# Fewer attention steps beside the input projection's last block, and the second feed-forward product's sums in the first product's tiles

## The chip, the cores and the metric

The kernel runs on one core of a Trainium2 chip. The metric is the device time of one execution in microseconds (us). An execution has five engines that run their own instruction streams in order: TensorE (PE, with its weight loads as PEld), VectorE (DVE), ScalarE (ACT), GpSimd (POOL) and SyncE (SP). Here SP issues the transfers between HBM and the on-chip memory.

## What is computed

One layer of a hybrid decoder on 2048 tokens of width 1024, in float32:

```
h = rms_norm(x, mix_norm_g);  P = h @ w_in
A = sliding_window_attention(...)   # 6 heads, window 128, blocks of 128 queries
B = rwkv7_mixer(...)                # a recurrence over the sequence
M = memory_attention(...)           # 4 heads against 256 memory tokens
x = x + concat(A, B, M) @ w_out
u = rms_norm(x, ffn_norm_g) @ w_up               # 1024 -> 2 * 2816
uc = conv_b + sum(conv_w[i] * shifted(u, i))     # causal, width 3
gate, val = split(uc)
x = x + (silu(gate) * val) @ w_down              # 2816 -> 1024
```

## The kernel before

Every float32 product is made of three matmuls of split operands: high part by high part, high by low, low by high. ACT makes the high part by a cast (`whi<-wraw`, `h2h<-tr`), DVE the low part by a subtraction (`wlo<-wraw,whi`, `h2l<-tr,h2h`). The tokens are worked on transposed, in blocks of 512 columns.

**Order of the work.** The program isn't issued as it is written. `Recorder` (line 132) records every operation; `slots` (line 212) lets a tile that takes a ring's place wait for the users of the tile that it replaces; `order` (line 239) gives every operation a level, the length of the longest path from it to the end by a table of costs, and `run` (line 269) then lists the operations of each engine, the highest level first among those that are ready. So the order in which steps are recorded acts through the rings of tiles (above all the PSUM ring `ip` of two places, which attention shares with the projection's statistics and transposes), and through the opening and closing of pools.

**First half of the kernel.** `ip` (line 677) is the input projection: four blocks of 512 tokens, 17 projections each, every one 24 matmuls `mm<-hh,...` of 512 columns, so 68 projections, counted by g. After each one `side(g)` (line 1546) advances two generators. `rw` is RWKV: 4 steps for each of 16 tiles of 128 tokens, at the projections that `starts` names, with a chain of 31 small DVE steps in each tile (`xtmp`, `xinv`). `atn` is attention (line 904): six steps for each of 16 tiles, 96 in all. Its matmuls write `pl`, `tpa` and `po` (window), `plm`, `tpm` and `pm` (memory). It may start once `x_done` has run, behind the last projection of the third block; from g = 52 on, the formula with 72 advances it by 72 steps over the last block's 16 projections, 12 tiles. What is left of it is recorded behind the projection, one step of `atn` and one of `rw` in turn (`run`, line 1485). `outproj` (line 1266) is recorded last: four blocks of eight projections (`mm<-ch,...`), each block from the attention and RWKV results of four tiles, with `ch` and `cl` in one place each.

**Second half.** `feed_forward` (line 1435) splits the tokens into two halves of 1024 columns. A product of a pair of weight rows is made by `seven` (line 1379): seven block products (sums in PSUM `uf`, `uip`, `uch`) in place of eight, with operands prepared by `operands` (line 1345) and seven slots of activations, `h2h` and `h2l`. `ffn_up` (line 1393) makes 22 such products for each half; DVE adds their sums into `ub`, then ACT and DVE make the convolution in `uc`, and DVE the gated product and its combinations in `uc` and `tt`, which SP writes to HBM (`dg`). All of these lie in the pool `fu`: three places `ub` of 1026 columns, five `uc` of 1024. `ffn_down` (line 1426) makes the second product: SP reads `dg` back (`tr<-dg`) into the slots, three stages of four calls for each half, and DVE adds each sum into `acc`, which is first loaded from `dx2`, the layer's sum so far, and written to `out` at the end of a half. `acc` is one tile of 8 x 1024 columns in a pool of its own, opened after `fu` is closed.

Of the kernel before, what the change touches and what calls it, by code (L numbers as in the profile page):

```python
# [10 lines left out]
F32 = mybir.dt.float32  # L11
# [7 lines left out]
P = 128  # L19
SEQ = 2048  # L20
D = 1024
KC = D // P
# [7 lines left out]
HALF = 2 * BLK  # L30
# [99 lines left out]
class Recorder:  # L130
# [15 lines left out]
    def pool(self, name, bufs, space=None, side=None):  # L146
        p = Pool_(name, bufs, space, side)
        self.pools.append(p)
        p.op = self.barrier[space] = self._mark("open", p, [self.barrier[space]] if space in self.barrier else [])
        self.stacks.setdefault((space, side), []).append(p)  # L150
        return p
# [72 lines left out]
    def margin(self, d, o):  # L224

        return 0 if d.eng == o.eng or None in (d.eng, o.eng) else MARGIN

# [33 lines left out]
    def run(self):  # L261
# [35 lines left out]
        while True:  # L297
# [17 lines left out]
            if soon[e] and o.dur > 150:  # L315
                c = min((c for c in soon[e] if c[0] < t + min(WAIT, o.dur) and c[2].level > o.level), default=None)
                if c:
# [41 lines left out]


WAIT = 100
MARGIN = 300
SLACK = 1500
WR = 4
# [4 lines left out]
UB = 3  # L369
# [44 lines left out]
class K:  # L414
# [1011 lines left out]
    def ffn_down(self, i, k0, nk, slots, w1, w2, ps, acc):  # L1426

        lo, hi = slice(0, BLK), slice(BLK, HALF)
        m1, m2 = acc[:, i], acc[:, i + 4]
        to = [(m1[:, lo],), (m1[:, lo],), (m1[:, hi],), (m2[:, hi],), (m2[:, hi],), (m1[:, hi],), (m2[:, lo],)]  # L1430

        def use(s, o):
            for c in to[s]:
                self.nc.vector.tensor_tensor(out=c, in0=o, in1=c, op=ALU.add)
        self.seven(ps, self.operands(w1, w2, lambda c, q: self.a["w_down"][i + 4 * c][:, (k0 + nk * q) * P:(k0 + nk * (q + 1)) * P]),
                   slots, nk, use)

    def feed_forward(self, ps):
        rec, pool, nc = self.rec, self.rec.pool, self.nc
        up = pool("fu", 1, side="right")  # L1440
        self.ucar = up.tile([P, 2 * NFC, 2], F32, name="ucar")
        nc.vector.memset(self.ucar, 0.0)
        w1, w2, tr = pool("fw1", 3), pool("fw2", 3), pool("fr", 3)
        slots = self.slots
        short = lambda: up.tile([P, BLK], F32, name="tt", bufs=4)
        wide = lambda name: up.tile([P, HALF], F32, name="uc", bufs=5)
        back = lambda: tr.tile([P, BLK], F32, name="tr")
        order = [k0 + q * nk + k for k0, nk in STAGES for k in range(nk) for q in range(2)]
        for half in range(2):
            if half:  # L1450
                self.from_dram(slots, 4, lambda k: self.dh[k], back)
            for n, j in enumerate(order):
                u = self.ffn_up(j, slots, w1, w2, up, ps)
                if n % 2:
                    self.to_dram(self.dg[half][n // 2], first, u, short)
                first = u
                if half == 0 and n == 7:
                    for k, r in self.normalised(1, wide):
                        self.to_dram(self.dh[k], *r, short)
        rec.close(up)  # L1460
        ap = pool("acc", 1, side="right")
        acc = ap.tile([P, KC, HALF], F32, name="acc")
        for half in range(2):
            col = slice(half * HALF, (half + 1) * HALF)
            for kc in range(KC):
                nc.sync.dma_start(out=acc[:, kc], in_=self.dx2[kc, :, col])
            pair = 0
            for k0, nk in STAGES:
                self.from_dram(slots, nk, lambda k: self.dg[half][pair + k], back)
                pair += nk  # L1470
                for i in range(4):
                    self.ffn_down(i, k0, nk, slots, w1, w2, ps, acc)
            for kc in range(KC):
                nc.sync.dma_start(out=self.out[kc * P:(kc + 1) * P, col], in_=acc[:, kc])
        for q in (ap, tr, w2, w1):
            rec.close(q)


    def run(self):
        tc, rec = self.tc, self.rec  # L1480
# [18 lines left out]
        pool = rec.pool  # L1499
# [44 lines left out]
        atn = []  # L1544

        def side(g):
            for _ in range(starts.get(g, 0)):
                next(rw, None)
            if atn and (g - 52) * 72 // 16 >= 0:
                for _ in range((g - 51) * 72 // 16 - (g - 52) * 72 // 16):  # L1550
                    next(atn[0], None)
        for n, b in (("t", 2), ("w", 4), ("h", 1), ("x", 4)):
            p[n] = pool(n, b, side="right")
# [2 lines left out]
        def x_done():  # L1556
# [3 lines left out]
            p["a"] = pool("a", 2)  # L1560
            atn.append(self.attention(p, ps))
        self.ip(p, ps, side, x_done)
        for n in ("h", "w", "t"):
            rec.close(p[n])
# [12 lines left out]
        wide = lambda name: rp.tile([P, HALF], F32, name=name, bufs=1 if name == "bc" else 2)  # L1577
# [117 lines left out]
```

## Time and profile before

| | |
|---|---|
| time, median of 3 runs | 2493.63 us (2492.27 to 2495.86) |
| the profiled execution | 2499.48 us |
| its span, first to last instruction | 2497.6 us |
| PE busy | 2372.4 us (95%) |
| PEld busy | 1886.0 us (76%) |
| DVE busy | 2015.2 us (81%) |
| ACT busy | 1219.6 us (49%) |
| POOL busy | 190.2 us (8%) |

Busy shares are of the span. A matmul's busy time holds its pipeline's latency, so matmuls that follow each other closely overlap in it. The "granted clock" is the share of TensorE's full clock in a stretch. A row's last part in brackets says how long the engine was idle before it and what ended that. All operations are recorded on one line (L349), so rows are told apart by their tiles.

### The profile page before, as it was taken

What the parts mean: (1) busy time and instruction counts of PE and PEld (TensorE: products, weight loads), DVE (VectorE), ACT (ScalarE), POOL (GpSimd) and SP (SyncE); (2) the same over time, 40 slices, a digit from 0 to 9 for tenths busy, and PEclk for the clock granted to TensorE, in tenths of its full rate; (3) what the DMA queues carried; (4) which work ended last, traced back from release to release, by engine and by line L of the source; (5) the groups of instructions that cost most, each with busy time, mean ns of one, the idle gap of its engine ahead of it and who ended that gap; (6) DMA issues with size and microseconds to landing.
All of it is one profiled execution on the core that took longest, in us unless ns stands there. A gap on an engine that the chain in (4) does not pass through costs nothing.

```text
span 2497.6 us, 36689 instructions
## 1 busy us (share of the span) xinstructions
PE 2372.4 (95%) x12268; PEld 1886.0 (76%) x12268; DVE 2015.2 (81%) x4614; ACT 1219.6 (49%) x2413; POOL 190.2 (8%) x292
## 2 busy tenths in 40 slices
PE   8899989899899979999899999999999998999999
PEld 6677777676666757777788888888888876888887
DVE  7579677878878777759588998899888887888876
ACT  6354544555445544555355455565555463444442
POOL 1112212211111121100000000000000000000000
PEclk9999999899989989999999999999999998999999
DMA  7586746744434465557233733354323246558443
GB/s 226 176 246 179 214 127 176 190 131 137 138 106 132 118 192 157 168 162 238 81 117 110 261 119 117 115 179 137 106 93 113 100 150 214 162 155 275 148 141 129
DMA packets 292933, 389.30 MB, mean 156 GB/s; under 512 B 49911, under 2 KB 155392, under 8 KB 292744
## 3 DMA queue, kind: packets, MB, share of 16 engines
q1 hardware_dynamic: 292744, 386.96, 49.8%
q8 instruction: 97, 1.59, 0.3%
q14 instruction: 92, 0.75, 0.1%
HBM read 274.89 MB, written 111.97 MB: 155 GB/s over the span
## 4 chain that ended last, share of the span: by engine, by line
PE 80%; DVE 8%; DMA 7%; issue 3%; ACT 1%; SPq 0%; POOL 0%; POOLq 0%; DVEq 0%; ACTq 0%
PE uf L349 28%; PE mm L349 16%; PE uch L349 14%; PE uip L349 7%; PE pq L349 4%; PE po L349 2%; PE pg L349 1%; DMA nb<-nbd 1%; PE tpa L349 1%; DVE xtmp L349 1%; DVE wlo L349 1%; PE pl L349 1%; PE st L349 1%; DVE xinv L349 1%; DMA wraw<-w_down_in 1%
## 5 line engine op out<-in xcount | busy, mean ns | idle before, releaser
L349 ACT CAST whi<-wraw 128x512 fp32r<-128x512 f32 (+1 forms) x410 | 250.2, 613 | 423.7 <-PE uf L349 148.9
L349 PE MATMUL uf<-h2h,wlo 128*128 128x512 f32 x1056 | 412.2, 392 | 15.3 <-DVE wlo L349 15.3
L349 PE MATMUL uf<-h2h,whi 128*128 128x512 f32 x1056 | 412.7, 392 | 4.7 <-ACT whi L349 4.6
L349 PE MATMUL uf<-h2l,whi 128*128 128x512 f32 x1056 | 412.6, 391 | 0.0
L349 DVE TENSOR_TENSOR wlo<-wraw,whi 128x512 fp32r<-128x512 f32 (+1 forms) x410 | 276.2, 677 | 89.1 <-ACT whi L349 87.7
L349 ACT CAST whi<-ws 128x512 fp32r<-128x512 f32 (+1 forms) x272 | 164.6, 609 | 288.5 <-PE uf L349 151.1
L349 DVE SCALAR_TENSOR_TENSOR uc<-ub,pp,uc 128x1024 f32<-128x1024 f32 x176 | 224.2, 1278 | 26.0 <-ACT uc L349 26.0
L349 PEld LDWEIGHTS uf<-h2h,wlo 128*128 128x128 f32 x1056 | 199.5, 189 | 59.0 <-DVE wlo L349 17.5
L349 PE MATMUL mm<-hh,whi 128*128 128x512 f32 x544 | 228.0, 420 | 15.6 <-DVE sh L349 5.4
L349 PEld LDWEIGHTS uf<-h2h,whi 128*128 128x128 f32 x1056 | 199.3, 189 | 48.4 <-ACT whi L349 6.4
L349 PEld LDWEIGHTS uf<-h2l,whi 128*128 128x128 f32 x1056 | 199.5, 189 | 41.8 <-DVE h2l L349 0.4
L349 PE MATMUL mm<-hl,whi 128*128 128x512 f32 x544 | 223.3, 411 | 2.0 <-DVE hl L349 1.9
L349 PE MATMUL mm<-hh,wlo 128*128 128x512 f32 x544 | 222.9, 410 | 0.0
L349 PE MATMUL uch<-h2h,whi 128*128 128x512 f32 x528 | 205.6, 389 | 0.0
L349 PE MATMUL uch<-h2h,wlo 128*128 128x512 f32 x528 | 205.5, 390 | 0.0
L349 PE MATMUL uch<-h2l,whi 128*128 128x512 f32 x528 | 205.4, 389 | 0.0
L349 DVE TENSOR_TENSOR wlo<-ws,whi 128x512 fp32r<-128x512 f32 (+1 forms) x272 | 178.5, 667 | 10.6 <-ACT whi L349 10.1
L349 PEld LDWEIGHTS mm<-hh,whi 128*128 128x128 f32 x544 | 106.6, 196 | 46.8 <-DVE sh L349 6.0
L349 ACT CAST h2h<-tr 128x512 fp32r<-128x512 f32 x182 | 110.0, 619 | 60.3 <-DMA tr<-dg 44.8
L349 ACT ACTIVATE uc<-ub,pp 128x1024 f32<-128x1024 f32 x88 | 109.4, 1244 | 38.4 <-DVE ub L349 37.1
L349 PEld LDWEIGHTS mm<-hl,whi 128*128 128x128 f32 x544 | 106.6, 196 | 25.8 <-DVE hl L349 3.4
L349 DVE TENSOR_TENSOR h2l<-tr,h2h 128x512 fp32r<-128x512 f32 x182 | 119.9, 684 | 7.3 <-ACT h2h L349 7.2
(363 smaller groups left out, 4702.8 us busy)
## 6 DMA issues: line engine op xcount, KB each, us to landing
wraw<-w_up_in SPq DMA_DIRECT2D x176, 256.0 KB
tr<-dg SPq DMA_DIRECT2D x154, 256.0 KB
wraw<-w_ip_in SPq DMA_DIRECT2D x136, 256.0 KB
dg<-uc SPq DMA_DIRECT2D x88, 256.0 KB
dg<-tt SPq DMA_DIRECT2D x66, 256.0 KB
wraw<-w_op_in SPq DMA_DIRECT2D x64, 256.0 KB
wraw<-w_down_in SPq DMA_DIRECT2D x64, 256.0 KB
xk<-xT_in SPq DMA_DIRECT2D x56, 256.0 KB
```

The costliest lines, as they stand in the source:

```text
L349: getattr(getattr(nc, o.eng), o.fn)(*map(real, o.a), **{k: real(v) for k, v in o.k.items()})
```

## The change

Two things. The number of attention steps that are recorded beside the last block's 16 projections is 48 instead of 72, so 8 tiles instead of 12; the other 48 are recorded behind the projection. And `fu` stays open to the end: `acc` is eight tiles of 1024 columns, three in places `ub` and five in places `uc`, recorded and loaded in the order 0, 4, 1, 5, 2, 6, 3, 7 (`ffn_down(i)` uses i and i + 4).

```diff
+EARLY = 48
+ACC_UB = (0, 3, 6)
@@ ffn_down
-        m1, m2 = acc[:, i], acc[:, i + 4]
+        m1, m2 = acc[i], acc[i + 4]
@@ feed_forward
-        rec.close(up)
-        ap = pool("acc", 1, side="right")
-        acc = ap.tile([P, KC, HALF], F32, name="acc")
+
         for half in range(2):
+            acc = [None] * KC
+            for n, kc in enumerate((0, 4, 1, 5, 2, 6, 3, 7)):
+                acc[kc] = up.tile([P, HALF + 2], F32, name="ub", bufs=UB)[:, 0:HALF] if n in ACC_UB else wide("acc")
             col = slice(half * HALF, (half + 1) * HALF)
-            for kc in range(KC):
-                nc.sync.dma_start(out=acc[:, kc], in_=self.dx2[kc, :, col])
+            for kc in (0, 4, 1, 5, 2, 6, 3, 7):
+                nc.sync.dma_start(out=acc[kc], in_=self.dx2[kc, :, col])
...
-                nc.sync.dma_start(out=self.out[kc * P:(kc + 1) * P, col], in_=acc[:, kc])
-        for q in (ap, tr, w2, w1):
+                nc.sync.dma_start(out=self.out[kc * P:(kc + 1) * P, col], in_=acc[kc])
+        for q in (up, tr, w2, w1):
@@ run, side(g)
-            if atn and (g - 52) * 72 // 16 >= 0:
-                for _ in range((g - 51) * 72 // 16 - (g - 52) * 72 // 16):
+            if atn and g >= 52:
+                for _ in range((g - 51) * EARLY // 16 - (g - 52) * EARLY // 16):
```

The planner makes a new order of it. PE before, around the output projection's first matmuls (`mm<-ch`; `pl` and `plm` are logits of attention):

```order
L349 MATMUL pm<-ptm,vm 64x128 x4
L349 MATMUL tpm_10329<-cst,em 128x128 x4
L349 MATMUL pm<-ptm,vm 64x128 x4
L349 MATMUL pl<-ka,dq 128x256 x10
L349 MATMUL mm<-ch,whi 128x512
L349 MATMUL mm<-cl,whi 128x512
L349 MATMUL pl<-ka,dq 128x256 x2
L349 MATMUL mm<-ch,wlo 128x512
```

The same place now (`pq` and `pg` are RWKV's):

```order
L349 MATMUL plm<-km,dq 128x256 x4
L349 MATMUL mm<-ch,whi 128x512
L349 MATMUL mm<-cl,whi 128x512
L349 MATMUL mm<-ch,wlo 128x512
L349 MATMUL mm<-ch,whi 128x512
L349 MATMUL mm<-cl,whi 128x512
L349 MATMUL tpm_9808<-cst,em 128x128 x2
L349 MATMUL pq<-uv,gmk 64x64 x6
L349 MATMUL tpm_9808<-cst,em 128x128 x2
L349 MATMUL po<-pt,va 64x384 x2
L349 MATMUL pg<-ar,bk 128x128 x6
L349 MATMUL mm<-ch,wlo 128x512
```

Before, 92 of the 128 `plm` stand ahead of the input projection's last matmul and 32 behind the output projection's first; now 60 do and 56. From the output projection's thirteenth projection on the two orders run alike.

DVE before, where `ffn_up` ends: the last convolutions (`uc<-ub,pp,uc`) and combinations (`tt`), and then the first low part of a `w_down` piece:

```order
L349 TENSOR_TENSOR ub<-uf,kt 128x512
L349 TENSOR_TENSOR h2l_12919<-tr,h2h_12901 128x512 x2
L349 TENSOR_TENSOR tt<-uc,tt 128x512
L349 SCALAR_TENSOR_TENSOR uc<-ub,pp,uc 128x1024
...
L349 SCALAR_TENSOR_TENSOR uc<-ub,pp,uc 128x1024 x4
...
L349 TENSOR_TENSOR tt<-uc,tt 128x512
L349 TENSOR_TENSOR wlo<-wraw,whi 128x512
L349 TENSOR_TENSOR h2l_12973<-tr,h2h_12955 128x512
```

DVE now, from the last `ub<-uf,kt` but one; the two `wlo<-wraw,whi` are those of the first two products with `w_down`:

```order
L349 TENSOR_TENSOR ub<-uf,kt 128x512
L349 TENSOR_TENSOR h2l_13018<-tr,h2h_12970 128x512
L349 TENSOR_TENSOR wlo<-ws,whi 128x512
L349 TENSOR_TENSOR ub<-uch,kt 128x512
L349 COPY ucar<-ub 128x2
L349 TENSOR_TENSOR wlo<-ws,whi 128x512
L349 TENSOR_TENSOR wlo<-wraw,whi 128x512
L349 COPY ucar<-ub 128x2
L349 TENSOR_TENSOR wlo<-wraw,whi 128x512
L349 TENSOR_TENSOR tt<-uc,tt 128x512
L349 SCALAR_TENSOR_TENSOR uc<-ub,pp,uc 128x1024
```

The first low parts for the second product now stand ahead of `ffn_up`'s last convolutions, which are spread among the first and second calls of `ffn_down`.

SP before, at the same place:

```order
L349 DMA dg_10_21156<-tt 128x512
L349 DMA acc<-dx__10585 128x1024
L349 DMA tr<-dg_2_14630 128x512
L349 DMA tr<-dg_3_14968 128x512
L349 DMA tr<-dg_0_13972 128x512
L349 DMA acc<-dx__10585 128x1024
```

And now:

```order
L349 DMA wraw<-w_down_in 128x512
L349 DMA ub<-dx__10102 128x1024
L349 DMA tr<-dg_2_14630 128x512
L349 DMA dg_9_20750<-uc 128x512
L349 DMA tr<-dg_3_14968 128x512
L349 DMA tr<-dg_0_13972 128x512
L349 DMA uc<-dx__10102 128x1024
```

The first two loads of sums stood behind all writes of `dg`; they now stand ahead of the last three writes of `dg_9` and of all seven of `dg_10`, or among them.

## Rows read from the trace of the kernel before

**Rows 1.** The page's head: span and instructions.
```profile
span 2497.6 us, 36689 instructions
```

**Rows 2.** Busy time by stretch: us from the span's start, length, engines.
```profile
core 0: us, PE busy (x) PEld busy (x) DVE busy (x) ACT busy (x) POOL busy (x), PEclk, DMA share, GB/s
277.00:453.00 176.00, 166.12 (x1097) 130.95 (x1096) 133.61 (x406) 80.49 (x179) 36.03 (x47) 0.96 0.54 160
453.00:891.00 438.00, 391.78 (x2694) 282.66 (x2693) 350.39 (x1354) 224.39 (x644) 77.98 (x128) 0.92 0.50 139
891.00:1100.00 209.00, 196.49 (x1252) 144.08 (x1252) 149.11 (x500) 106.99 (x276) 27.82 (x57) 0.95 0.54 160
1100.00:1202.00 102.00, 96.08 (x405) 77.46 (x403) 78.11 (x120) 47.36 (x83) 1.39 (x1) 0.93 0.65 209
1211.00:2030.00 819.00, 816.55 (x3580) 673.32 (x3580) 720.66 (x1110) 427.27 (x630) 0.00 (x0) 0.99 0.38 127
2050.00:2091.00 41.00, 28.02 (x111) 22.24 (x110) 39.27 (x62) 20.08 (x31) 0.00 (x0) 0.83 0.75 260
2091.00:2290.00 199.00, 199.00 (x878) 164.28 (x877) 160.39 (x269) 81.09 (x142) 0.00 (x0) 1.00 0.56 177
```

**Rows 3.** The same stretches, projections' matmuls alone (tile mm).
```profile
277.00:453.00 176.00, 106.48 (x408) 0.96 0.54 160
453.00:891.00 438.00, 128.32 (x408) 0.92 0.50 139
891.00:1100.00 209.00, 108.19 (x384) 0.95 0.54 160
```

**Rows 4.** Attention's matmuls plm alone, eight a tile.
```profile
453.00:891.00 438.00, 18.68 (x96) 0.92 0.50 139
891.00:1100.00 209.00, 6.70 (x32) 0.95 0.54 160
```

**Rows 5.** RWKV's first matmul pz (one a tile), then its last, pgt (two).
```profile
277.00:453.00 176.00, 1.18 (x3) 0.96 0.54 160
453.00:891.00 438.00, 4.01 (x9) 0.92 0.50 139
891.00:1100.00 209.00, 0.45 (x1) 0.95 0.54 160
...
277.00:453.00 176.00, 2.10 (x6) 0.96 0.54 160
453.00:891.00 438.00, 5.31 (x16) 0.92 0.50 139
891.00:1100.00 209.00, 3.53 (x10) 0.95 0.54 160
```

**Rows 6.** The chain of waits, a stretch of the first product: start, length.
```profile
1224.60 5.44 PE uf L349 x24
```

**Rows 7.** PE in order of time where the first product ends: start, length.
```profile
2057.17 0.39 PE L349 MATMUL uip<-h2l,whi 128*128 128x512 f32 x1
2070.46 0.80 PE L349 MATMUL uf<-h2h,wlo 128*128 128x512 f32 x1 [12.90 <-DVE wlo L349]
```

**Rows 8.** DVE in order of time in that gap.
```profile
2058.77 4.86 DVE L349 SCALAR_TENSOR_TENSOR uc<-ub,pp,uc 128x1024 f32<-128x1024 f32 x4
...
2069.12 0.68 DVE L349 TENSOR_TENSOR tt<-uc,tt 128x512 f32<-128x512 f32 x1
2069.72 0.68 DVE L349 TENSOR_TENSOR wlo<-wraw,whi 128x512 fp32r<-128x512 f32 x1
```

**Rows 9.** The chain of waits, transfers behind that gap: start, length.
```profile
2070.33 3.29 DMA dg<-tt
2073.74 4.53 DMA acc<-dx__10585
```

**Rows 10.** Transfers of 2050 to 2091 us: GB/s in 40 slices, and their sum.
```profile
GB/s 0 256 236 288 134 284 300 38 76 296 148 0 0 0 16 228 346 262 340 382 396 394 196 0 140 212 318 398 422 344 388 406 410 378 354 412 414 396 394 396
DMA packets 5107, 10.65 MB, mean 260 GB/s; under 512 B 560, under 2 KB 560, under 8 KB 5105
```

## The prediction

> **What bounds the kernel now.** I read the busy time by stretch first, because the kernel has stages with different limits. From 1211 us on PE is nearly full: 816.6 of 819 us busy and a granted clock of 0.99 [rows 2], and the chain shows 24 matmuls in 5.44 us, 0.227 us each [rows 6]. A change that takes work off another engine is worth nothing there; only a place where PE stands still can be won. There is one, where the first feed-forward product ends: 12.90 us idle until DVE's `wlo` [rows 7]. In the 41 us around it PE ran 111 matmuls [rows 2], which are 25.2 us at 0.227 us; so 15.8 us are lost, the gap itself and some 3 us behind it partly at the lower of the clock's two levels, 1.2 instead of 2.4 GHz (0.83 granted in the mean of the stretch).
>
> DVE in that gap shows why: it is busy 39.3 of the 41 us, and runs the first product's last convolutions and combinations (from 2058.8 us) until 2069.7 us before it comes to the `wlo` [rows 8]. SP has a wait of its own right behind: the load of the sums waits 3.29 us for a write of `dg` to land, and lands 4.53 us later [rows 9]. The transfers stood still for about 3 us near 2062 us and ran at 340 to 420 GB/s afterwards [rows 10].
>
> In the first half no engine is full. The last block of the input projection, 453 to 891 us, has PE busy 0.89, DVE 0.80 and a clock of 0.92; the first half of the output projection, to 1100 us, 0.94, 0.71 and 0.95 [rows 2]. Attention is in both: 96 of the 128 `plm` (12 tiles) in the first, 32 (4 tiles) in the second [rows 4].
>
> **Term 1, four attention tiles move.** By the order, four tiles go from the block into the stretch behind it. Nothing is removed; what counts is what a tile costs at either place. I work it out from elapsed time. A projection is 24 matmuls, 5.44 us [rows 6]. The block before attention (277 to 453 us) has 408 matmuls of projections, 17 projections or 92.5 us [rows 3], and three RWKV tiles (3 `pz`, 6 `pgt` [rows 5]); the other 83.5 us give at most 27.8 us for an RWKV tile. The last block has 17 projections [rows 3], 8.5 RWKV tiles (mean of 9 `pz` and 16 `pgt`) and 12 of attention: 438 - 92.5 - 236.3 leaves 109 us, **9.1 us a tile**. The stretch behind has 16 projections, 87.0 us, three RWKV tiles and four of attention: 209 - 87.0 - 83.4 leaves 38.6 us, **9.6 us a tile**. If an RWKV tile costs half as much beside other work, 13.9 us, attention costs 18.9 us and 20.1 us. Either way the two places cost the same within 1.2 us, so the move costs 2 to 5 us by this. Against that stands the clock: it is 0.92 in the block with 12 tiles and 0.96 in the one without [rows 2]; a third of the tiles gone brings it a third of the way, 1.3% of some 350 us, 5 us. I take **-2 us**. The ends, with the prices crossed: leaves at 18.9 and arrives at 9.6, -37 us; leaves at 9.1 and arrives at 20.1, +44 us. By the order RWKV also comes forward by one to two tiles, into blocks that have nothing but projections beside it; I cost that at nothing, since it pays the 27.8 us there that I take for it in the block as well. The later 20 output projections stand as before.
>
> **Term 2, the sums lie in the first product's tiles.** No computation is removed; there are as many loads, adds and writes. What goes is the order in which all of `fu` had to be done first. I count DVE's work from the same sum on both sides (the last `ub<-uf,kt` but one) to the first `wlo` of `w_down`, at 0.60 us for 512 columns and 1.2 us for 1024 [rows 8]. Before: 23 of 512 and 10 of 1024, 26 us. Now: 6 of 512, 3.7 us. PE waited 12.9 us for it [rows 7], so would have wanted it at 13 us; now PE comes to it 14 matmuls (3.2 us) earlier in its order, at 10 us, and it is there. What is late next is the end of the first call's seven products: the order puts PE's last matmul of them 122 matmuls, 27.7 us, behind that, at 38 us; DVE's last piece for it stands behind 52 of 512 and 7 of 1024, 39.9 us. So 2 to 3 us stay lost, and I take a **gain of 13 us** of the 15.8. What is put off (five passes of 1024 columns and four of 512, 8.4 us) lies under DVE's idle 38.6 of the next 199 us [rows 2]; without that cover it would come back whole.
>
> The transfers are the other limit. 10.65 MB went in the 41 us [rows 10]; if PE stands still for none of it they must go in 25.2 us, 423 GB/s. At 396 GB/s, a usual slice of those rows, they need 26.9 us: a gain of 14.1 us at most. The Trainium skill, DMA: Bandwidth & Descriptors, section "Where 436 GB/s comes from", sets about 358 GB/s as the HBM limit of a core; by that figure an estimate is 29.7 us and a gain of 11.3 us. The rows, at 380 to 420 for some 15 us, do not agree with it here. The ends of this term: nothing won, and 15.8 us.
>
> **Sum.** The profiled execution took 2499.48 us, 1.9 us more than its span [rows 1] and 5.85 us more than the runs' median. -2 and -13 give 2484.5 us for it, and 2478.6 us beside the median of 2493.63: I forecast **2479 us**. Some 0.2%, 5 us, is what a measurement can tell from no change.
>
> **Rivals.**
> *A, the two kinds of work mix better than prices say.* Weight loads are busy 0.645 of the last block, 0.689 of the stretch behind it and 0.82 of the full stretch from 1211 us [rows 2]: PE has room in both. If both ran at 0.689, 426.7 us of weight loads would take 619 us instead of 647, 28 us less; with term 2, 2453 us. For it: DVE and PE are both short of full in the block. Against: the equal prices above. The Trainium skill, Perfetto Trace Analysis, section "Optimization Strategy", says that stages with different busiest engines can gain from being interleaved, which is this rival; the rows bear it out only in part, since PE is the busier of the two engines in both stretches.
> *B, a new wait takes the old one's place.* SP issues in order. Five of the eight sums now lie in places `uc` whose last reader is a write of `dg`, and such a write took 3.29 us to land [rows 9]; four such waits ahead of `tr` and `wraw` loads are 13 us. Then term 2 gives 0 to 5 us: about 2489 us. For it: the new order has a load of a sum a row or two behind such writes. Against: between them stand operands for other products, and PE's order mixes products of two calls.
> *C, slower: attention arrives dearer than it leaves.* If the last block is bound by RWKV and DVE's chain, a tile gives back only 9.1 us on leaving. Behind the projection it has only 16 projections beside it, since the third output block waits for the places of `ch` and `cl` and for tile 11. Above a difference of 4.5 us a tile the kernel is slower in spite of term 2. An arrival half-way between 9.6 and 20.1 gives +23 - 13, 2504 us; the full 20.1 gives +44 - 13, 2525 us.
> *D, the change does not do what it says*, because the planner sorts anew: excluded by the order, in which 32 `plm` have moved and the loads of sums stand ahead of `dg_10`.
>
> **Chances.** Forecast (2468 to 2488 us) 0.52, A 0.17, B 0.17, C 0.14. The range leaves out C and the outer part of A: 2450 to 2497 us. Faster by over 0.2% is the forecast, A and a small part of B: 0.72; within 0.2%, most of B and the mildest C: 0.15; slower 0.13.
>
> **What would show it.** In the new profile the gap in front of the first `w_down` product should be under 3 us and the clock there near 1, with `uc<-ub,pp,uc` on DVE behind the first adds into the sums. The time from the first input projection of the last block to the first output projection should fall by some 40 to 90 us, and the first half of the output projection should grow by about as much. I am wrong if PE waits on `tr`, `wraw` or a sum's load behind 2057 us, or if these two stretches differ by more than 20 us in sum.

## The result and the profile after

The changed kernel took 2459.51 us (median of 4 runs, 2456.57 to 2462.42), beside 2494.74 us (4 runs, 2492.27 to 2498.06) of the kernel before: ratio 0.9857, 95% interval 0.9842 to 0.9871. It is faster by 35 us where 15 were forecast; the time lies inside the range of 2450 to 2497 us. The profiled execution of the change took 2456.57 us, at the lower end of its runs, and that of the kernel before 2499.48 us, above its runs; so the two profiles differ by 43 us, 8 more than the medians.

The page's head and busy times of the kernel after (before: 36689 instructions [rows 1] and PE 2372.4 us busy):

```profile
span 2454.7 us, 36671 instructions
...
PE 2361.2 (96%) x12268; PEld 1876.8 (76%) x12268; DVE 2007.0 (82%) x4614; ACT 1217.6 (50%) x2413; POOL 184.4 (8%) x292
```

Busy time by stretch, kernel after, the stretches that answer to [rows 2]: the third block of the input projection, its last block, the first 16 output projections, the first feed-forward product, the change between the products, and the second one:

```profile
core 0: us, PE busy (x) PEld busy (x) DVE busy (x) ACT busy (x) POOL busy (x), PEclk, DMA share, GB/s
303.00:478.00 175.00, 161.90 (x1033) 125.31 (x1031) 136.05 (x433) 78.65 (x173) 40.66 (x63) 0.98 0.52 156
478.00:817.00 339.00, 318.17 (x2190) 236.74 (x2187) 276.47 (x1043) 182.36 (x515) 61.84 (x101) 0.92 0.54 157
817.00:1067.00 250.00, 234.44 (x1540) 168.70 (x1540) 189.13 (x672) 136.03 (x377) 29.13 (x59) 0.98 0.50 153
...
1177.00:1996.00 819.00, 816.33 (x3581) 673.23 (x3581) 721.07 (x1111) 427.52 (x631) 0.00 (x0) 1.00 0.37 127
2016.00:2057.00 41.00, 38.65 (x160) 30.18 (x159) 40.07 (x62) 23.24 (x37) 0.00 (x0) 0.96 0.73 244
2057.00:2256.00 199.00, 197.26 (x863) 160.84 (x862) 166.17 (x278) 83.85 (x146) 0.00 (x0) 1.00 0.61 195
```

Attention's `plm` alone, kernel after, in the last block and in the stretch behind it (96 and 32 in [rows 4]; columns as above without POOL), and PE in order of time where the two meet:

```profile
478.00:817.00 339.00, 14.02 (x68) 11.16 (x69) 11.61 (x17) 20.58 (x68) 0.92 0.54 157
817.00:1067.00 250.00, 11.48 (x60) 8.98 (x60) 10.24 (x15) 18.28 (x60) 0.98 0.50 153
```

```profile
817.01 0.72 PE L349 MATMUL plm<-km,dq 128*128 128x256 f32 x4
817.57 0.39 PE L349 MATMUL mm<-ch,whi 128*128 128x512 f32 x1
```

Read together: four of the 60 stand just behind 817.0 us and still ahead of the first output projection (817.57 us), so 72 `plm`, nine tiles, lie in the last block where 96 lay: 24 `plm`, **three tiles**, left it. Behind the input projection's last matmul there are four tiles more than before, as the prediction has it, but one of the four still runs ahead of the first output projection. The block shrank from 438 to 339 us, 99 us less; the stretch that took them grew from 209 to 250, 41 us more. RWKV tiles came forward by the new order as well, so the second block, 118 us before by PE's rows in order of time, is now 144; the third stayed (175). Up to the first matmul of the feed-forward stage the kernel needs 1176.6 us where it needed 1210.5: **34 us** come from the first half. The stage itself takes 1278.1 us where it took 1287.1: **9 us** come from the sums. Together that is the 43 us of the two profiles; how the 35 us of the medians divide is measured below, 28 and 12.5 us.

The instructions of the first half are the same (some 6724 matmuls in both). So the 34 us can be split into PE's idle time and the time that the same matmuls were busy, which differs only by the clock and by how they overlap. Windows from the start to the feed-forward stage, kernel before and kernel after:

```profile
0.00:1210.50 1210.50, 1105.84 (x6724) 842.30 (x6724) 914.79 (x2879) 596.79 (x1447) 190.22 (x292) 0.94 0.57 167
```

```profile
0.00:1176.60 1176.60, 1094.27 (x6724) 834.92 (x6724) 907.50 (x2879) 594.78 (x1447) 184.42 (x292) 0.96 0.57 172
```

Idle went from 104.7 to 82.3 us, 22 less; busy from 1105.8 to 1094.3, 12 less, with the granted clock up from 0.94 to 0.96. In the last block itself the clock stayed at 0.92; behind it, it rose from 0.95 to 0.98. Where PE waited in the last block is in the waits of PE there (us in total, times, longest), first before, then after:

```profile
PE pl L349 <- DVE lg L349: 10.4, 6, 3.9
PE tpa L349 <- DVE lg L349: 5.7, 3, 3.0
PE mm L349 <- DVE sh L349: 4.1, 1, 4.1
PE mm L349 <- DVE kp L349: 2.7, 1, 2.7
```

```profile
PE mm L349 <- DVE sh L349: 3.4, 2, 2.5
PE po L349 <- ACT pt L349: 3.0, 2, 1.7
...
PE pl L349 <- DVE lg L349: 1.2, 1, 1.2
...
PE tpa L349 <- DVE lg L349: 0.9, 2, 0.7
```

Attention's own waits for DVE's `lg` (the logits that DVE takes out of PSUM) fell from 16 us to 2, while PE's idle time in the block fell from 46 to 21.

### The profile page after: what moved, and what is told of

The parts are those of the page before. It is cut to its first block, busy times and chain, and to the rows that moved or that the text cites. A ratio compares the mean times of both kernels' runs of the same rounds, so it can differ in the third digit from the quotient of the medians.

```text
span 2454.7 us, 36671 instructions
## 1 busy us (share of the span) xinstructions
PE 2361.2 (96%) x12268; PEld 1876.8 (76%) x12268; DVE 2007.0 (82%) x4614; ACT 1217.6 (50%) x2413; POOL 184.4 (8%) x292
## 4 chain that ended last, share of the span: by engine, by line
PE 77%; DVE 11%; DMA 6%; issue 4%; ACT 2%; SPq 0%; POOL 0%; POOLq 0%; DVEq 0%; ACTq 0%
PE uf L349 27%; PE mm L349 15%; PE uch L349 13%; PE uip L349 7%; PE pq L349 4%; PE po L349 2%; PE pg L349 2%; DMA nb<-nbd 2%; DVE wlo L349 1%; DMA tr<-dg 1%; DVE uc L349 1%; PE tpa L349 1%; DVE h2l L349 1%; PE pl L349 1%; DVE lg L349 1%
```

## The experiments

Theories. **Prices** (the prediction's): an attention tile costs the same at both places. **Crowding**: the last block held more work beside its projections than it could hide, so tiles that leave it give back more than they cost elsewhere. **RWKV**: the gain comes from the RWKV tiles that the new order happens to bring forward. **Details**: every order draws PE's idle time and its slow stretches anew, and the change drew well. Tiles of a kernel are counted in its order; an RWKV tile by its matmuls `pq`. The expectations name the boundaries of the RWKV counts one too early: where they say "in front of projection 17, 34 and 51" it is 34, 51 and 60, and the counts for the block hold.

### The two parts apart

```diff
-            if atn and (g - 52) * 72 // 16 >= 0:
-                for _ in range((g - 51) * 72 // 16 - (g - 52) * 72 // 16):
+            if atn and g >= 52:
+                for _ in range((g - 51) * 48 // 16 - (g - 52) * 48 // 16):
```

> The change's part in the attention alone; the sums of the second product lie in a pool of their own as before. By the prediction's term 1 (an attention tile costs the same at both places): 2 us less than the kernel before, within 5 us. Crowding theory (a tile that leaves the crowded last block gives back about 27 us and costs about 14 us where it arrives): 26 us less, 20 to 34. RWKV theory (the gain comes from the one to two RWKV tiles that the planner brought forward in the same order): also 26 us less, since this kernel has them as well. If the two parts of the change help each other, less than 20 us here.

Measured: 2469.11 us beside 2497.22, 28 us less; ratio 0.9889 (0.9868 to 0.9909). The other part, with everything of the diff except that the steps stay at 72:

```diff
+EARLY = 72
```

> The change's part in the sums alone; attention steps at 72 per 16 projections as before. The prediction's term 2: 13 us less than before. The two profiles (feed-forward stage 1291.0 us before, 1282.0 us after): 9 us less. Were the two parts of the change to help each other, more than 15 us would be missing from the sum of this run and the one with the attention alone against the whole change's 35 us.

Measured: 2484.70 beside 2497.22, 12.5 us less; 0.9947 (0.9928 to 0.9965). In the profile the feed-forward stage took 1277.8 us, 9.3 less than before, with the same first half (1210.5). (The expectation begins the stage 3.9 us earlier, hence its 1291.0 and 1282.0; the difference is the same.) Together 40.6 us, the whole change 35: the parts add up within their intervals, and neither needs the other. Prices is out by 26 us; the term of the sums holds.

### RWKV's place

Every operation's level can be raised by `rec.boost` ns, an addition that the planner's code has already. Raised around RWKV's steps it moves RWKV alone:

```diff
+            rec.boost = 100
             for _ in range(starts.get(g, 0)):
                 next(rw, None)
+            rec.boost = 0
```

> The kernel before, attention in its old places (12 tiles in the last block), but RWKV steps get 100 ns more of the planner's level, by which 2, 5 and 8 of 16 RWKV tiles are done in front of projection 17, 34 and 51, as after the change, in place of 0.3, 4 and 7.3. RWKV theory: about 26 us less than before. Crowding by attention alone: within 5 us of before. Crowding by all work beside the block's projections: in between, about 27 us for each of the 0.7 tiles that leave the last block less what they cost earlier, so 5 to 12 us less.

Measured: 2483.34 us, 14 less than before; 0.994 (0.992 to 0.996). More than attention alone allows, and half of what RWKV by itself should give. The profiled execution is 10 us below the median, so its stretches serve only roughly: the block took 385 us with 12 attention and 7 RWKV tiles, 53 less than with 8.

The mirror, in the kernel with the attention part alone:

```diff
+            rec.boost = -200 if g < 34 else 0
             for _ in range(starts.get(g, 0)):
                 next(rw, None)
+            rec.boost = 0
```

> The mirror of the run before: attention's steps as the change has them (9 tiles in front of the first output projection), but RWKV steps up to projection 34 get 200 ns less of the planner's level, so that 1 and 4 of 16 RWKV tiles are done in front of projection 17 and 34, as before the change (0.3 and 4), in place of 2 and 5. Crowding by attention: 26 us less than before, as with the attention alone. RWKV theory: within 8 us of before.

Measured: 2460.05 us, 37 less than before and 11 more than forecast; 0.985 (0.9827 to 0.9872). The gain does not need RWKV forward: the RWKV theory is out as the cause. Beside the attention-only run this prices an RWKV tile once attention has thinned out: the block went from 339.7 to 360.6 us for one tile more, and the two blocks ahead of it from 321.5 to 300.6 us for one fewer: 21 us in either place. By this one pair of orders, RWKV's place matters only while the block is crowded.

Further forward, attention as before (`rec.boost = 1000` in place of 100):

> The kernel before, attention in its old places (12 tiles in the block), RWKV with 1000 ns more of the planner's level: 4, 8 and 10.8 of 16 tiles in front of projections 17, 34 and 51 (0.3, 4 and 7.3 before), so that the block holds 5 RWKV tiles in place of 8. RWKV theory, on the line of the smaller shift (14 us for 0.7 tiles out of the block): over 30 us less than before. Crowding by attention alone: within 10 us of before. Crowding by all work in the block: 15 to 35 us less.

Measured: 2477.16 beside 2494.64, 17.5 less; 0.993 (0.9907 to 0.9954). Three tiles out of the block give little more than one. What they give back in the block they cost in the blocks ahead (364 us where 294 stood), where PE now waits 8.5 us for ACT's `hh`.

### How many attention tiles

All with the sums as changed, and only `EARLY` other than 48:

```diff
-EARLY = 48
+EARLY = 60
```

> The whole change with 60 steps of attention per 16 projections in place of 48: 10 attention tiles in front of the first output projection by the order (9 in the change, 12 before), 12 of RWKV. Crowding theory, linear from 12 tiles (2484.7 us with the sums alone) to 9 (2459.5 us), 8.4 us a tile: 2468 us. Planner's luck (the order of the change happens to fit): anywhere from 2455 to 2490 us, not in line.

Measured: 2459.85 us beside 2496.93; 0.9855 (0.982 to 0.9891), the same as with 48. So the gain is not 8.4 us for each tile; of the two forecasts it fits the second, "not in line", and the reading by stretches that follows was made afterwards:

| kernel | tiles in the last block: attention, RWKV | last block, us | first 16 output projections, us |
|---|---|---|---|
| sums only | 12, 8 | 438.1 | 208.1 |
| 60 steps | 10, 7.7 | 375.5 | 229.5 |
| attention only, RWKV late | 9, 7.8 | 360.6 | 247.5 |

With RWKV about level, the eleventh and twelfth attention tiles cost the block 31 us each, and 11 each behind it; the tenth costs 15 in the block and 18 behind it. The 31 us are an upper bound: 0.3 of an RWKV tile left with them, and at the 53 us that the whole tile gave above, an estimate, that is 16 of the 63 us, which leaves 23 us a tile. **The last two tiles were dear, the one before them was not**, by one order for each count.

```diff
-EARLY = 48
+EARLY = 36
```

> The whole change with 36 steps: 6.5 attention tiles and 10 RWKV tiles in front of the first output projection. If a tile that leaves the block goes on giving 8.4 us net: 2459.5 less 2.5 x 8.4, 2438 us. If the block is no longer crowded at 9 tiles and the stretch behind it becomes so: over 2460 us.

```diff
-EARLY = 48
+EARLY = 24
```

> The whole change with 24 steps: 4.5 attention tiles and 9 RWKV tiles in front of the first output projection, 11.5 and 7 behind. Linear: 2459.5 less 4.5 x 8.4, 2422 us. Crowding on both sides (an optimum between): over 2470 us, with the stretch of the output projections as short of PE as the last block was.

Measured: 2480.44 us with 36 (0.9945; 0.9919 to 0.9971) and 2438.87 us with 24 (0.9763; 0.9729 to 0.9796), beside 2496.93. Both sides of 48, out of any line: 36 fits its second forecast, 24 neither. The ten runs with 36 steps lie from 2471.91 to 2496.22 us, and the profiled one is 11 us above their median. The windows to the feed-forward stage, 36 steps, then 24:

```profile
0.00:1212.80 1212.80, 1119.77 (x6725) 851.48 (x6725) 910.21 (x2879) 592.74 (x1447) 179.05 (x292) 0.94 0.56 167
```

```profile
0.00:1165.70 1165.70, 1084.94 (x6724) 829.86 (x6724) 909.23 (x2879) 595.29 (x1447) 186.95 (x292) 0.96 0.58 174
```

Of the 47 us between these two executions (42 between the medians) 35 are busy time of the same matmuls, with the clock at 0.94 and 0.96, and 12 are idle.

Fewer tiles of RWKV in the block of the whole change (`rec.boost = 1000` around its steps, as above):

> The whole change, and RWKV steps with 1000 ns more of the planner's level: 4, 8 and 11 of 16 RWKV tiles in front of projection 17, 34 and 51 (2, 5 and 8 in the change), 8.5 tiles of attention and 12.7 of RWKV in front of the first output projection, so that the last block holds 4.7 RWKV tiles in place of 6.8. Crowding by all work in the block: 3 tiles leave it for blocks that hold only projections; at some 21 to 27 us given back and some 25 us taken there, 0 to 15 us less than the change. RWKV theory (each tile brought forward gains about 14 us net): 30 us less than the change.

Measured: 2444.81 beside 2496.93; 0.9787 (0.9757 to 0.9817), 15 us below the change.

### Counts or details

Nearly the same tiles in the same blocks, sorted anew by a constant of the planner. Two of the kernel before:

```diff
-MARGIN = 300
+MARGIN = 297
```

> The kernel before with the planner's margin between engines at 297 ns in place of 300: the same counts of RWKV and attention tiles at every boundary, but the instructions of the first half sorted anew in detail. If the number of attention tiles in the block makes the change's gain: within 5 us of before. If such a gain hangs on the details of an order (the fixed work is the same; the idle time of PE and the stretches at the lower clock are drawn anew with every order): anywhere within some 25 us of before, to either side.

```diff
-WAIT = 100
+WAIT = 104
```

> The kernel before with the planner's wait for a more urgent instruction at 104 ns in place of 100: again the same counts, another order in detail. Counts decide: within 5 us of before. Details decide: anywhere within some 25 us of it.

Measured beside 2497.96: 2495.55 (0.9992; 0.9981 to 1.0004) and 2501.88 us (1.0013; 1.0 to 1.0027). Two of the change, with `MARGIN = 303` and with `WAIT = 104`:

> The whole change with the planner's margin at 303 ns: 8.5 to 9 attention tiles in front of the first output projection as in the change, another order in detail. Counts decide: within 5 us of the change's 2459.5 us. Details decide: anywhere from 2440 to 2485 us.

> The whole change with the planner's wait at 104 ns: 9 attention tiles in front of the first output projection, RWKV counts as in the change, another order in detail. Counts decide: within 5 us of the change's 2459.5 us. Details decide: anywhere from 2440 to 2485 us.

Measured: 2444.07 (0.9781; 0.9765 to 0.9797) and 2462.62 us (0.985; 0.9824 to 0.9875). And the two odd ones, 36 and 24 steps with `MARGIN = 303`, and 24 steps with RWKV forward (`rec.boost = 1000`):

> The whole change with 36 steps, as in the run that gave 2480 us, and the planner's margin at 303 ns: the same counts (6.5 attention and 10 RWKV tiles in front of the first output projection), another order in detail. Counts decide: 2475 to 2486 us. Details decide: nearer to the line between 48 steps (2460 us) and 24 (2439 us), 2440 to 2465 us.

> The whole change with 24 steps, as in the run that gave 2439 us, and the planner's margin at 303 ns: 4.5 attention and 9 RWKV tiles in front of the first output projection. Counts decide: within 6 us of 2439 us. Details decide: up to 2465 us.

> The whole change with 24 steps, and RWKV with 1000 ns more of the planner's level: 4.5 attention and 12 RWKV tiles in front of the first output projection, 4 and 8 RWKV tiles in front of projections 17 and 34. If both gains add up (24 steps gave 21 us below the change, RWKV forward 15): 2424 us. If both take the same crowding away: 2435 to 2445 us.

Measured beside 2494.64: 2464.60 (0.9879; 0.9861 to 0.9897), 2449.43 (0.9832; 0.981 to 0.9854) and 2456.45 us (0.9847; 0.983 to 0.9864). What follows:

- With 12 attention and 8 RWKV tiles in the block, three orders gave 2496 to 2502 us.
- With fewer, the time no longer follows the count. The same counts in two orders differ by 3 us with 48 steps (2459.51 and 2462.62), 16 with 36 and 11 with 24. The run of 2444.07 us belongs to 48 steps as well, but the block holds 8.5 attention and 6.3 RWKV tiles there in place of 9 and 6.8, so its 15 us are not detail alone.
- The three orders of the kernel before are a mild trial of "Details": in PE's order of the first half 8% and 5% of the matmuls moved by more than ten places, against 20% and 39% with 36 and 24 steps, and 6% in the order that changed 48 steps by 3 us.
- The wider comparison is better. Five orders keep 12 attention tiles in the block, two of them with RWKV moved and so sorted quite anew (in one, 68% of the matmuls moved by more than ten places): by the medians they stand from 4 us above the kernel before to 17.5 below it. Six orders have 8.5 to 10 tiles: less the 12.5 us of the sums where they have them, they stand 23 to 41 us below. The groups do not overlap, so the number of attention tiles counts; where in its group a kernel falls, the order decides.
- The gains do not add up: 24 steps and RWKV forward together took 2456.45 us, above both forecasts and 7 to 18 us above 24 steps alone. So "both take the same crowding away" is not shown either. In this order one attention tile stands behind the sixteenth output projection, and from there to the feed-forward stage the kernel took 129.5 us where it takes 110.5 with 24 steps alone.

### What is left at the change of products

```diff
+                    rec.boost = 8000 if half == 0 and k0 == 0 and i < 2 else 0
                     self.ffn_down(i, k0, nk, slots, w1, w2, ps, acc)
```

> The whole change, and 8000 ns more of the planner's level for the first two calls of the second product, so that DVE comes to their weight sums some rows earlier; the first half of the kernel is ordered as in the change. If DVE's order at that place is what keeps the rest of the loss: the feed-forward stage of the profile falls from 1278.1 us by 3 to 5 us. If DVE has simply too much to do there (41.9 of 43 us busy): the stage stays within 2 us of 1278.1 us, and PE waits for something else of DVE's.

Measured: 2465.59 us beside 2497.06 (0.9874; 0.9858 to 0.9891). The stage took 1283.1 us in place of 1278.1, which neither forecast had: the waits of 0.92 and 0.80 us at this place went, but others came. PE in order of time, this run:

```profile
2042.59 0.50 PE L349 MATMUL uf<-h2h,whi 128*128 128x512 f32 x1 [1.54 <-ACT h2h L349]
...
2078.71 0.79 PE L349 MATMUL uch<-h2h,whi 128*128 128x512 f32 x1 [3.61 <-ACT whi L349]
```

Precedence for these sums is no cure here; other operands are late in this run. That DVE simply has too much to do is not shown either, since DVE was busy less here (76.8 of the 90 us from 2000, 83.3 in the change). What would take away the rest stays open.

## Why the prediction was right and wrong

**What bounds the kernel: right.** Only PE's standing still could be won, and it was: in the two profiles PE's idle time and its slow stretches make up the whole gain.

**Term 2, the sums: right in kind, some 3 us too large by the profile.** Forecast 13 of the 15.8 us. The gap of 12.90 us [rows 7] is gone; the clock in the same 41 us rose from 0.83 to 0.96. From 2000 to 2090 us PE ran 370 matmuls, 84 us at 0.227 us, so 6 us are lost and about 10 won. The stage agrees: 1285 to 1287 us in seven kernels without the new sums, 1269 to 1280 in eleven of the twelve with them (1283 in the run that gives the weight sums precedence); the median of the sums alone says 12.5. What is late next is what the prediction named, DVE's pieces for the first calls, but they cost 6 us, not the "2 to 3 us" of the step. PE, then ACT and DVE in order of time, kernel after, and the stretch behind the two gaps:

```profile
2041.85 0.50 PE L349 MATMUL uch<-h2h,whi 128*128 128x512 f32 x1 [0.92 <-ACT whi L349]
...
2043.67 0.50 PE L349 MATMUL uf<-h2h,whi 128*128 128x512 f32 x1 [0.80 <-ACT whi L349]
2044.01 0.94 PE L349 MATMUL uf<-h2l,whi 128*128 128x512 f32 x2
```

```profile
2043.00 0.62 ACT L349 CAST whi<-ws 128x512 fp32r<-128x512 f32 x1 [0.68 <-DVE ws L349]
```

```profile
2041.02 1.27 DVE L349 SCALAR_TENSOR_TENSOR uc<-ub,pp,uc 128x1024 f32<-128x1024 f32 x1
2042.21 0.68 DVE L349 TENSOR_TENSOR ws<-ws,wraw 128x512 f32<-128x512 f32 x1
```

```profile
2044.10:2047.50 3.40, 3.40 (x10) 2.67 (x9) 3.40 (x6) 0.57 (x2) 0.00 (x0) 0.50 0.37 119
```

One of the passes put off (`uc<-ub,pp,uc`) runs ahead of the sum of weights `ws` that ACT's `whi` and so PE wait for. The step compared when DVE's last piece ends with when PE's last matmul of the call ends (39.9 against 38 us); but PE waits at every operand on the way, and behind two gaps of under 1 us it ran 3.4 us at the lower clock, its matmuls 0.43 us apart.

**Term 1, the attention tiles: wrong, and the step is the price.** "Either way the two places cost the same" took an average over all tiles, "9.1 us a tile" in the block against "9.6 us" behind it, for what the tiles that leave cost. The move alone gave 28 us where the term had 2: what leaves is the last of twelve. With RWKV about level, the last two cost at most 31 us each in the block and 11 behind it; the third, 15 and 18, is about as even as the prediction had it.

That the averages are equal was not measured either; it hangs on how RWKV's tiles are counted. The prediction counted first and last matmuls, 3, 8.5 and 3 tiles in the three stretches. By `pq`, 60 matmuls a tile and the count of the experiments, it is 3.7, 8 and 4. Kernel before, `pq` alone:

```profile
277.00:453.00 176.00, 24.13 (x222) 19.30 (x222) 7.09 (x15) 0.96 0.54 160
453.00:891.00 438.00, 53.63 (x480) 43.15 (x480) 15.18 (x32) 0.92 0.50 139
891.00:1100.00 209.00, 27.08 (x240) 21.57 (x240) 7.59 (x16) 0.95 0.54 160
```

The same working then has 83.5 / 3.7 = 22.6 us for an RWKV tile, and for an attention tile 13.7 us in the block against 7.9 behind it: so three tiles would win some 17 us, an estimate from the same rows. By RWKV's chain on DVE (`xtmp`, 165, 521 and 183 of the 992 instructions, so 2.7, 8.4 and 3.0 tiles) it is 6.8 and 7.3 us, about even again. Rows that give 5.8 us or nothing by the choice of a count cannot carry a price to 1.2 us. The crossed end that pointed this way, -37 us, was written down, and set aside for the equal averages. The number of tiles was off too: three crossed into the stretch behind, not four. And the 5 us for the clock were to come from the block, a third of the way from 0.92 to 0.96; the block stayed at 0.92.

**The tiles of RWKV that come forward: "at nothing" holds in a thinned block** (21 us in either place), not in a crowded one: out of the old block one tile and the new order were worth 14 us.

**Rival A was the case.** It put both stretches at a weight-load share of 0.689 and took 28 us from that. Attention alone gave 28.1 us, and in the change the shares are 236.74 of 339 and 168.70 of 250, together 0.688. That it comes so near is in part luck: the orders with 8.5 to 10 tiles lie 23 to 41 us below the kernel before without the sums. It stood at 0.17 because equal average prices spoke against it; the shares of PE busy, 0.89 and 0.94 with the clock at 0.92 and 0.95 [rows 2], had already said that elapsed time in the block buys less work than behind it. The Trainium skill, Perfetto Trace Analysis, section "Optimization Strategy", says that where the busiest engine changes over time, interleaving those stages may improve the time. The 28 us agree in part, since PE is the busier engine in both stretches; with fewer than 10 tiles in the block, more spreading gave no steady gain.

**Rivals B, C and D** did not come about: no wait of over 1 us stands in PE's rows behind 2016 us (ACT waits there 9.8 us for `tr<-dg`, but PE at most 0.9 us for ACT), and arrival cost 41 us against 99. Of the 32 `plm` that D names, 24 crossed the first output projection.

**What was to show it.** The gap is under 3 us, `uc<-ub,pp,uc` stands behind first adds into the sums: as said. The block was to fall by 40 to 90 us and fell by 99, the stretch behind to grow by as much and grew by 41; "more than 20 us in sum" was named as what would make it wrong, and it is 58, of which 25 came back in the blocks ahead.

## What to carry to other kernels

An average price of a piece of work need not be what the last piece costs in a stretch where the engine that counts neither is full nor at its clock. Read the idle time and the granted clock of both stretches, count the other work there in two ways, and where the averages disagree let the price stand as a range. In a kernel whose order a planner makes, measure a change under two or three orders with the same counts before a gain of 10 us is put down to it. Once the crowding is gone, the best order found is a draw: 24 steps gave 2438.87 us here, 21 us below the change, and 2449.43 us under another margin.

## What was not expected of the hardware

The clock fell with no gap in PE's busy time. In the run with 36 steps PE is busy for every microsecond from 696 to 720 us, yet at the lower of its two levels (1.2 in place of 2.4 GHz) from 704 to beyond 716 us. Windows of 4 us, and PE in order of time, of that run:

```profile
696.00:700.00 4.00, 4.00 (x19) 3.34 (x18) 3.83 (x17) 2.20 (x9) 0.00 (x0) 1.00 0.21 46
700.00:704.00 4.00, 4.00 (x27) 2.66 (x28) 1.72 (x3) 2.23 (x5) 1.03 (x4) 1.00 0.86 288
704.00:708.00 4.00, 4.00 (x27) 2.99 (x25) 2.05 (x8) 0.80 (x2) 1.04 (x4) 0.50 0.79 201
708.00:712.00 4.00, 4.00 (x27) 3.33 (x27) 2.59 (x7) 3.19 (x13) 0.51 (x1) 0.50 0.34 86
712.00:716.00 4.00, 4.00 (x9) 1.85 (x8) 3.43 (x13) 0.16 (x1) 0.82 (x1) 0.50 0.18 29
716.00:720.00 4.00, 4.00 (x19) 3.03 (x18) 0.47 (x1) 1.09 (x2) 0.54 (x1) 0.80 0.21 53
```

```profile
700.06 0.39 PE L349 MATMUL mm<-hh,wlo 128*128 128x512 f32 x1
700.38 0.33 PE L349 MATMUL pu<-qa,X 64*64 64x64 f32 x4
700.64 0.39 PE L349 MATMUL plm<-km,dq 128*128 128x256 f32 x1
700.95 0.33 PE L349 MATMUL pu<-qa,X 64*64 64x64 f32 x2
...
703.35 1.73 PE L349 MATMUL pg<-ar,bk 64*128 64x128 f32 x12
...
705.41 1.73 PE L349 MATMUL pq<-uv,gmk 64*64 64x64 f32 x12
...
712.30 0.79 PE L349 MATMUL mm<-hh,whi 128*128 128x512 f32 x1
712.89 0.63 PE L349 MATMUL mm<-hl,whi 128*128 128x512 f32 x1
```

From 700.4 us on, ahead of the fall and while it lasted, PE ran only small matmuls (64 to 256 columns), most of them RWKV's and attention's, with none of the projection's 512 columns between; the projection's matmuls came back at 712 us, 0.43 to 0.6 us apart. But such work does not always bring a fall. The kernel after has a stretch of the same kind, from 713.0 to 724.7 us, all small matmuls (64 to 384 columns) and as busy, and the clock stayed at the higher level (kernel after, then the run with 36 steps):

```profile
713.00:725.00 12.00, 12.00 (x75) 8.09 (x75) 8.17 (x31) 5.08 (x12) 0.00 (x0) 1.00 0.37 116
```

```profile
700.00:712.00 12.00, 12.00 (x75) 8.97 (x74) 6.35 (x16) 6.22 (x19) 2.58 (x9) 0.67 0.66 192
```

Both have 75 matmuls in 12 us, and PE's busy time is modelled and holds the pipeline's latency, so it does not tell them apart. What made the clock fall in the one stretch stays open, and so does how much of the dear 36 steps comes from such falls; no run takes it apart.
